# Quarter tiles of the input's block sums at a pitch of 320 columns, and five buffers instead of six in the weight rings

## The chip, the cores and the metric

The kernel runs on one core of one Trainium2 chip. The metric is the device time of one execution in microseconds (us). TensorE (PE in the profile) multiplies matrices, VectorE (DVE), ScalarE (ACT) and GpSimd (POOL) do elementwise work, and SyncE (SP) issues nearly all DMA transfers. Each engine has an instruction stream of its own, which it works off in order; semaphores order the streams against each other. On-chip memory has two parts: SBUF, the working memory of all engines, in which each of the 128 partitions holds a row of bytes, and PSUM, into which TensorE writes its sums.

## The reference

One step of a one-layer streaming encoder, for a prompt of 512 frames and a sample of 32 frames of a running stream. Both go through the layer as one matrix of 544 columns (`T`). Cut to what matters:

```python
xn   = rmsnorm(h, norm_g)
proj = xn @ w_in            # 1024 -> 3*2048 + 8 + 4*1024 + 2*1024 columns
u, v_m, z_m, ig, fg, q_h, f_h, i_h, g_h, ga, gb = split(proj)
c  = silu(causal_conv(u))                       # mLSTM branch, 4 heads of 512
qm, km = c @ w_qm, c @ w_km * 512 ** -0.5       # per head
hm = mlstm(qm, km, v_m, ig, log_sigmoid(fg), C0, n0, m0)
ya = ((layernorm(hm) + m_skip * c) * silu(z_m)) @ w_brm
oh = hgrn(silu(q_h), f_h, i_h, S0)              # HGRN2 branch, 8 heads of 128
yb = (rmsnorm(oh) * silu(g_h)) @ w_brh
h  = h + (sigmoid(ga) * ya + sigmoid(gb) * yb) @ w_out
h  = h + sigmoid(h @ w_pg) * (p @ w_ple)
y  = rmsnorm(h, final_g)                        # and the new states
```

All of it is in float32, and the states are outputs too.

## The kernel before

**Products.** A float32 product is made of three passes over operands that are split into a high and a low part (`fp32r`): high times high, high times low, low times high. So each weight piece of 128 x 512 (four weight blocks of 128 x 128) exists three times in SBUF: as it was loaded (`wr`, "raw"), its high part (`wh`, a copy by ScalarE) and its low part (`wl`, raw minus high by VectorE). Each kind has a ring of buffers, `NRAW` and `NPIECE` of them, six each. A ring is handed out when the program is built: a new piece takes a buffer that an older piece has given up, and the instruction that fills it waits until the older piece's last reader is done. For a raw piece that is a DMA in SyncE's queue, for a high piece a copy on ScalarE, for a low piece a subtraction on VectorE.

**Seven products for eight.** The big projection `w_in` and the output product `w_out` run over pairs of 128-column units (`class Two`; `Onto` for `w_out`) by Strassen's scheme in Winograd's form: seven block products, called a11, s2, a12, s3, s1, a22, s4, in place of eight. Each is 12 matmuls of 272 columns (four weight blocks, three passes each; 272 is `TH`, half of 544). Four of the seven (s1, s3, a22, s2) multiply with sums of blocks of the input. Those sums are made once, by `xf_sums` (line 365): for each of four pairs of input rows one tile of high parts and one of low parts, each with four quarters of 272 columns. Quarter 0 is for s1, 1 for s3, 2 for a22 and 3 for s2 (`moving`, line 528). The other three products read halves of the normalized input itself (`xh`, `xl`).

**Memory.** The rings and tiles are laid out in SBUF pool by pool, in the order of the lines at the function's head: constants `cp`, weight rings `wp`, the pair tiles `xp`, slots `sp`, small tiles `tp`. The pair tiles have two rings (tags x0 and x1) of four buffers, each of 4352 bytes per partition before, which is four quarters of 1088 bytes. In the built program the first of them begins 224 bytes past a multiple of 256, and 4352 and the sizes before it keep that for all eight. So the quarters begin 224, 32, 96 and 160 bytes past a multiple of 256. The same tiles hold other operands at other times (`pair_tile`, line 141): the raw input at the start, the first head's queries, the HGRN2 output ahead of `w_brh` and `h` ahead of `w_pg`; there the high part takes the first half and the low part the second.

**Stages.** Start and first projections (to about 60 us in the profile); four mLSTM heads (to about 590 us), each with keys and queries (`stage_k`, `stage_q`), scores, the chain of memory and output (`mchain`) and the product with `w_brm` (`stage_br`), between which a `Pump` places the blocks of the next projections; eight HGRN2 heads (to about 880 us), whose chain of levels is interleaved with further blocks; the merge gates; then `w_brh`, `w_out`, `w_pg` and the output.

**What sets the order.** TensorE's order is written out by hand from beginning to end. At the start and in the HGRN2 stage ScalarE's and VectorE's are too. In the mLSTM heads, in the merge's tail and for SyncE throughout, a scheduler that runs when the program is built places the instructions; it knows the rings, so a different number of buffers makes a different order. Once built, the order is fixed.

In the heads, the weights of a block are split three blocks ahead (`AHEAD`), and the results of a block leave PSUM through `keep` (line 563, a copy on ScalarE, names t...) or `put` (line 569, on VectorE or ScalarE). For the units of the convolution input `u` the target is a tile `ub`, whose convolution starts on ScalarE (`conv_first`, line 764) and goes on with three taps on VectorE (`conv_rest`, line 772, names cv...).

Of the kernel before, what the change touches and what calls it, by code (L numbers as in the profile page):

```python
# [20 lines left out]
NP = 512  # L21
T = NS + NP
TH = T // 2
MH = 4
HD = 512
KH = HD // P
# [27 lines left out]
NSLOT = 26  # L54
NEVAC = 8
WP = 512
NRAW = 6
NSUM = 4
NPIECE = 6
AHEAD = 3  # L60
SCRATCH = 1024
RAWAHEAD = 3
# [18 lines left out]
def hybrid_step(ctx: ExitStack, tc: tile.TileContext, a, o):  # L81
# [2 lines left out]

    cp = ctx.enter_context(tc.tile_pool(name="cp", bufs=1))
    wp = ctx.enter_context(tc.tile_pool(name="wp", bufs=NPIECE))
    xp = ctx.enter_context(tc.tile_pool(name="xp", bufs=KD // 2))
    sp = ctx.enter_context(tc.tile_pool(name="sp", bufs=NSLOT))
    tp = ctx.enter_context(tc.tile_pool(name="tp", bufs=2))
    psum = {}  # L90

    def aux_pool(name, bufs):
# [47 lines left out]

    def pair_tile(name, ring):

        t = xp.tile([P, 2 * T], F32R, tag=f"x{ring}", name=name)
        return t[:, :T], t[:, T:]

    def psplit(src, name, ring):
        hi, lo = pair_tile(name, ring)
# [117 lines left out]
    def rms_cols(acc, blocks, name, pc=None):  # L265

        pc = pc or paux(name + "pc")
        n = len(blocks)
        st = small("rms_s", [P, 8])
        V.memset(st[:, :n], 1.0)  # L270
        for i, (t0, m) in enumerate(blocks):
            PE.matmul(pc[:m, 0, 2 * i : 2 * i + 2], acc[:, t0 : t0 + m], ones, start=True, stop=True)
        i = 0
        while i < n:
            j = i
            while j < n and blocks[j][1] == blocks[i][1]:
                j += 1
            m = blocks[i][1]
            V.tensor_scalar(st[:m, i:j], pc[:m, 0, 2 * i : 2 * j : 2], 1.0 / D, EPS, ALU.mult, ALU.add)
            i = j  # L280
        r = small("rms_r", [P, 8])
        rsqrt(r[:, :n], st[:, :n], P, n)
        return r
# [81 lines left out]
    def xf_sums(k):  # L365

        ring = f"x{int(k in (1, 2))}"
        h = xp.tile([P, 4, TH], F32R, tag=ring, name=f"xfh{k}")
        l = xp.tile([P, 4, TH], F32R, tag=ring, name=f"xfl{k}")
        u = cp.tile([P, T], F32, tag="lm", name=f"xu{k}")  # L370
        x11, x12 = u[:, one], u[:, other]
        x21, x22 = (tp.tile([P, TH], F32, tag="half", name=f"xv{k}{b}", bufs=3) for b in range(2))
# [596 lines left out]
    def stage_q(h, u):  # L969
# [21 lines left out]
        if u:  # L991

            with tc.issue_after(read.ins):
                S.activation(small("silu", [1, 2]), ident[:1, :2], AF.Silu)
        return low

    def stage_scores(h):
# [327 lines left out]
    def hgrn_bounds(decayed, masked):  # L1325

        l0, l1 = vec[:, V_LB : V_LB + HH], vec[:, V_LB + HH : V_LB + 2 * HH]
        lm, le = small("lbm", [P, HH]), small("lbe", [P, 2, HH])
        with tc.issue_after(masked.ins):
            V.tensor_tensor(lm, l0, l1, ALU.max)  # L1330
            V.tensor_tensor(le[:, 0, :], l0, lm, ALU.subtract)
# [834 lines left out]
```

## Time and profile before

| | |
|---|---|
| three timed runs | 1117.81, 1118.29, 1118.54 us, median 1118.29 |
| profiled execution, first to last instruction | 1116.3 us |
| TensorE busy | 1108.7 us (99%), 8825 matmuls (8507 in the program; a product of plain float32 shows as two) |
| VectorE, ScalarE, GpSimd busy | 922.1, 714.8, 158.4 us |
| granted TensorE clock | 1.000 |
| DMA | 135.78 MB, mean 122 GB/s |

The profile has only the span of its execution; that execution's own time is not listed apart from it. The median of the timed runs is 2.0 us above the span, which is what lies before the first and after the last instruction. "Busy" counts the time from an instruction's start to its end. Matmuls overlap in the pipeline: one takes about 290 ns from start to end, but the next starts about 125 ns after it. So a TensorE that is 99% busy can still run slower or faster, and the time from one start to the next is what has to be read. In the timeline view a row is: start in us, duration in us, engine, line, operation, tiles written and read, shape, count, and in brackets the idle time ahead of it and what ended that.

### The profile page before, as it was taken

How to read it: one execution, taken by the hardware profiler on the slowest of the kernel's cores; microseconds unless marked ns; L12 is line 12 of the kernel's file. 1: busy time of each engine (PE TensorE's matmuls, PEld its weight loads, DVE VectorE, ACT ScalarE, POOL GpSimd, SP SyncE). 2: the span in 40 equal slices, each digit the busy share in tenths (PEclk: the TensorE clock that was granted, in tenths of full speed). 3: DMA queues.
4: the chain of work that ended last, by engine and by line, in shares of the span. 5: the costliest groups of instructions: out<-in, count | busy, mean ns of one | idle time of the engine just before them, and what ended most of it. 6: DMA issues, size and time to landing. Idle time of an engine off the chain costs nothing.

```text
span 1116.3 us, 23756 instructions
## 1 busy us (share of the span) xinstructions
PE 1108.7 (99%) x8825; PEld 1097.3 (98%) x8825; DVE 922.1 (83%) x1969; ACT 714.8 (64%) x1583; POOL 158.4 (14%) x412
## 2 busy tenths in 40 slices
PE   9999999999999999999999999999999999999998
PEld 9999999999999999999999999999999999999998
DVE  6986998676896786986898699999999888789785
ACT  6686657754666555664667478787777776445662
POOL 5112021101010110101200123222322000000000
PEclk9999999999999999999999999999999999999999
DMA  6234225232264132461556322122222353333943
GB/s 224 77 95 128 86 67 176 96 114 96 74 215 157 39 124 104 131 222 53 195 176 206 107 77 83 56 84 74 84 75 74 109 166 114 111 125 103 304 150 119
DMA packets 78044, 135.78 MB, mean 122 GB/s; under 512 B 8804, under 2 KB 16612, under 8 KB 77928
## 3 DMA queue, kind: packets, MB, share of 16 engines
q1 hardware_dynamic: 77760, 134.21, 36.9%
q8 instruction: 69, 1.13, 0.4%
q14 instruction: 47, 0.39, 0.1%
q10 hardware_dynamic: 168, 0.06, 0.0%
HBM read 109.32 MB, written 24.91 MB: 120 GB/s over the span
## 4 chain that ended last, share of the span: by engine, by line
PE 94%; DVE 3%; ACT 1%; DMA 1%; issue 1%; SPq 0%; ACTq 0%; DVEq 0%
PE d L549 42%; PE ya L199 9%; PE pg L2017 4%; PE yb L199 4%; PE k L199 4%; PE q L199 4%; PE C L1069 3%; PE pl L1741 3%; PE u L326 2%; PE sc L1012 2%; PE v L199 2%; PE nm L1248 2%; PE d L431 1%; PE ple L199 1%; PE yt L1290 1%; PE ho L1855 1%
## 5 line engine op out<-in xcount | busy, mean ns | idle before, releaser
L566 ACT COPY t<-d 128x272 f32<-128x272 f32 x126 | 47.4, 376 | 5.2 <-PE d L549 5.0
L1762 DVE TENSOR_TENSOR hkq<-hkq,hq 128x288 f32<-128x288 f32 (+1 forms) x96 | 41.5, 439 | 5.6 <-PE pl L1741 2.5
L1696 ACT COPY km<-hkq 128x256 f32<-128x256 f32 x56 | 23.9, 427 | 30.5 <-DVE hkq L1762 28.4
L1741 PE MATMUL pl<-hkq,km 128*128 128x128 f32 x224 | 37.9, 291 | 0.6 <-ACT km L1696 0.6
L774 DVE SCALAR_TENSOR_TENSOR cv<-ub,vec,cv 128x547 f32<-128x547 f32 x48 | 37.0, 781 | 0.4
L1741 PEld LDWEIGHTS pl<-hkq,km 128*128 128x128 f32 x224 | 30.9, 190 | 2.7 <-ACT km L1696 1.6
L1177 DVE SCALAR_TENSOR_TENSOR c<-c,wi,Cs 128x258 f32<-128x258 f32 x32 | 15.1, 477 | 20.2 <-PE Cs L1175 20.1
L1081 ACT COPY Co<-C 128x258 f32<-128x258 f32 x30 | 9.8, 379 | 28.3 <-PE C L1069 20.7
L1316 DVE TENSOR_TENSOR y<-ya,y 128x272 f32<-128x272 f32 x48 | 18.8, 432 | 8.8 <-PE ya L199 8.7
L1776 DVE COPY_PREDICATED at<-lmask,pl 128x256 f32<-128x256 uint8 (+1 forms) x56 | 25.3, 452 | 0.3
L1259 ACT COPY y<-nm 128x516 f32<-128x516 f32 x16 | 9.4, 589 | 18.0 <-PE nm L1248 17.8
L1026 ACT CAST sh<-dm 128x512 fp32r<-128x512 f32 (+3 forms) x16 | 7.4, 459 | 20.4 <-DVE dm L1020 20.4
L939 POOL COPY vsm<-vt 128x96 f32<-128x96 f32 x16 | 7.2, 462 | 87.4 <-ACT vt L577 44.3
L1069 PE MATMUL C<-vh,kwh 128*128 128x258 f32 x96 | 19.3, 283 | 0.0
L1069 PE MATMUL C<-vh,kwl 128*128 128x258 f32 x96 | 19.3, 282 | 0.0
L1069 PE MATMUL C<-vl,kwh 128*128 128x258 f32 x96 | 19.3, 282 | 0.0
L1012 PE MATMUL sc<-q,kh 128*128 128x512 f32 (+3 forms) x80 | 18.6, 320 | 0.1
L1207 DVE BATCH_NORM_STATS2 bs<-y 128x6 f32<-128x512 f32 (+1 forms) x20 | 13.7, 687 | 5.1 <-ACT y L1259 5.0
L963 DVE TENSOR_TENSOR kl<-kf,kh 128x512 fp32r<-128x512 f32 x16 | 11.0, 686 | 8.1 <-ACT kh L962 8.0
L767 POOL COPY uo<-ub 128x3 f32<-128x3 f32 x16 | 7.6, 472 | 64.1 <-DVE ub L573 39.3
L1248 PE MATMUL nm<-vh,sh 128*128 128x258 f32 x80 | 16.5, 288 | 0.0
L1768 POOL TENSOR_TENSOR hq<-hq 128x136 f32<-128x136 f32 (+4 forms) x40 | 16.0, 399 | 3.1
(4666 smaller groups left out, 5119.2 us busy)
## 6 DMA issues: line engine op xcount, KB each, us to landing
ya_d<-y SPq DMA_DIRECT2D x32, 272.0 KB, 3.0
y<-ya_d SPq DMA_DIRECT2D x24, 272.0 KB, 3.8
c<-in_C SPq DMA_DIRECT2D x16, 258.0 KB, 4.5
out_Cs<-c SPq DMA_DIRECT2D x16, 258.0 KB, 2.8
out_Cp<-Co SPq DMA_DIRECT2D x15, 258.0 KB, 2.4
x<-in_xT SPq DMA_DIRECT2D x8, 272.5 KB, 4.7
ya<-ya_d SPq DMA_DIRECT2D x8, 272.0 KB, 4.8
h<-in_xT SPq DMA_DIRECT2D x8, 272.0 KB, 2.8
```

The costliest lines, as they stand in the source:

```text
L199: PE.matmul(both[b][:m, :TH], part(w, off + k * step, m, x), xx[:, half(b)], start=(k == 0 and j == 0), stop=(k == n - 1 and j == 2),)
L549: PE.matmul(ps, ww[:, c], xx, start=(start and k == 0 and j == 0), stop=end, skip_group_check=not start,)
L566: S.copy(t, ps)
L774: last = V.scalar_tensor_tensor(cv[:, :547], ub[:, j : j + 547], vcol(V_CW + 4 * ft + j), cv[:, :547], ALU.mult, ALU.add)
L1012: PE.matmul(pn[:, 0, :n], ks[f][x][:, j * P : (j + 1) * P], qs[f][y][:, NS + j * P : T], start=(f == 0 and i == 0), stop=(f == KH - 1 and ...
L1069: PE.matmul(pn[g][:, :VH], kw[b][x][:, f * P : (f + 1) * P], vv[b][y][:, g * VH : (g + 1) * VH], start=(b == 0 and j == 0), stop=(b == NB ...
L1248: PE.matmul(pn[:, g, :VH], st[j][x][:, (i - j) * P : (i - j + 1) * P], vv[j][y][:, g * VH : (g + 1) * VH], start=(j == 0 and q == 0), stop ...
L1696: S.copy(km.rearrange("p (n j c) -> p n j c", j=2, c=c), view(kk, HB, ((2 * c, NA // (2 * c)), (c - HB, 2), (1, c))),)
L1741: PE.matmul(pn[:, b * P : (b + 1) * P], km[:, b * P : (b + 1) * P], view(qq, b * P, ((2 * c, P // (2 * c)), (HB + c, 2), (1, c))), start=True,
L1762: V.tensor_tensor(x, x, t, ALU.mult)
L1776: V.copy_predicated(at[:, :n], lmask[:, li, :n], pn[:, :n])
L2017: PE.matmul(ps, part(w, k * P, P, x), xx[:, c], start=(k == 0 and j == 0), stop=(k == KD - 1 and j == 2))
```

## The change

Quarters of the block sums get a pitch of 320 columns (1280 bytes) instead of 272; only 272 of the 320 are used. The pair tiles become 5120 bytes for it, 8 x 768 = 6144 bytes more per partition. The three weight rings give up one buffer of 2048 bytes each, which is 6144 bytes too. A tile of 48 columns (192 bytes), used by nothing, stands between the weight rings and the pair tiles, and four small tiles get one buffer instead of two. In the built program the first pair tile now begins 160 bytes past a multiple of 256, and since 1280 and 5120 are multiples of 256, so does each quarter of each of the eight tiles. Where a pair tile holds a high and a low half, they stay back to back, so their four halves begin at 160, 224, 32 and 96 instead of 224, 32, 96 and 160. The weight rings keep their place (224 past a multiple of 256).

```diff
+TW = 320
...
-NRAW = 6
+NRAW = 5
...
-NPIECE = 6
+NPIECE = 5
...
     wp = ctx.enter_context(tc.tile_pool(name="wp", bufs=NPIECE))
+    gp = ctx.enter_context(tc.tile_pool(name="gp", bufs=1))
     xp = ctx.enter_context(tc.tile_pool(name="xp", bufs=KD // 2))
...
+    gp.tile([P, 48], F32, name="gap")
...
     def pair_tile(name, ring):
 
-        t = xp.tile([P, 2 * T], F32R, tag=f"x{ring}", name=name)
-        return t[:, :T], t[:, T:]
+        t = xp.tile([P, 4 * TW], F32R, tag=f"x{ring}", name=name)
+        return t[:, :T], t[:, T : 2 * T]
...
-        st = small("rms_s", [P, 8])
+        st = small("rms_s", [P, 8], bufs=1)
...
-        h = xp.tile([P, 4, TH], F32R, tag=ring, name=f"xfh{k}")
-        l = xp.tile([P, 4, TH], F32R, tag=ring, name=f"xfl{k}")
+        h = xp.tile([P, 4, TW], F32R, tag=ring, name=f"xfh{k}")[:, :, :TH]
+        l = xp.tile([P, 4, TW], F32R, tag=ring, name=f"xfl{k}")[:, :, :TH]
...
-                S.activation(small("silu", [1, 2]), ident[:1, :2], AF.Silu)
+                S.activation(small("silu", [1, 2], bufs=1), ident[:1, :2], AF.Silu)
...
-        lm, le = small("lbm", [P, HH]), small("lbe", [P, 2, HH])
+        lm, le = small("lbm", [P, HH], bufs=1), small("lbe", [P, 2, HH], bufs=1)
```

No instruction is added or removed, and the order of the 8507 matmuls that the program issues is the same. On VectorE, ScalarE, GpSimd and SyncE the order differs in the mLSTM heads and around the merge's tail. In the built program's order the rows below read: line, operation, tile written <- tiles read with their buffer numbers, elements. The changed file's line numbers are three higher there, and its buffer numbers four.

The first place is on VectorE, among the projections that run beside the end of the second head (`h` = 1), near 314 us of the profile. Names: `ws310` is the weight sum for block s3 of units 10 and 11 and `ws310l` its low part, `ws110l` that for s1; `ub8` and `ub10` are convolution tiles that take results from PSUM (`d81`, `d101`), `cv8` is a convolution tap, `hm7l` a low part of the head's output. Before:

```order
L175 TENSOR_TENSOR wa1210l_4624<-wi10r1_4464,wa1210h_4623 128x512
L482 TENSOR_TENSOR ws310_4643<-wi10r0_4371,wi11r0_4373 128x512
L138 TENSOR_TENSOR hm7l_4573<-c7_2856,hm7h_4572 128x544
L573 TENSOR_TENSOR ub8_4385<-d81_4384,t168_4462 128x272
L175 TENSOR_TENSOR ws310l_4646<-ws310_4643,ws310h_4645 128x512
L175 TENSOR_TENSOR ws110l_4664<-ws110_4576,ws110h_4663 128x512
L573 TENSOR_TENSOR ub10_4586<-d101_4585,t110_4604 128x32
L573 TENSOR_TENSOR ub10_4586<-d101_4585,t110_4604 128x240
L774 SCALAR_TENSOR_TENSOR cv8_4682<-ub8_4385,vec_80,cv8_4682 128x547
```

and now:

```order
L178 TENSOR_TENSOR wa1210l_4628<-wi10r1_4468,wa1210h_4627 128x512
L141 TENSOR_TENSOR hm7l_4577<-c7_2860,hm7h_4576 128x544
L485 TENSOR_TENSOR ws410_4631<-ws210_4582,wi10r1_4468 128x512
L576 TENSOR_TENSOR ub8_4389<-d81_4388,t168_4466 128x272
L485 TENSOR_TENSOR ws310_4647<-wi10r0_4375,wi11r0_4377 128x512
L576 TENSOR_TENSOR ub10_4590<-d101_4589,t110_4608 128x32
L576 TENSOR_TENSOR ub10_4590<-d101_4589,t110_4608 128x240
L777 SCALAR_TENSOR_TENSOR cv8_4686<-ub8_4389,vec_84,cv8_4686 128x547
L178 TENSOR_TENSOR ws310l_4650<-ws310_4647,ws310h_4649 128x512
L178 TENSOR_TENSOR ws110l_4668<-ws110_4580,ws110h_4667 128x512
```

The sum `ws310` moved behind the first read of `d81`, and both reads of `d101` and a convolution tap moved ahead of `ws310l` and `ws110l`. The same rows moved in the same way in the third head for units 14 and 15 (`ws314l`, `ub12`, `ub14`, `cv12`).

The second place is on VectorE too, in the first head's queries near 88 us. `kl` are low parts of the keys, `q0` and `q1` those of the queries (each a read of PSUM), `col` and `cols` copies of small transposes out of PSUM, `wq010l` and `wq011l` the low parts of the next query weights, and `emc` a small copy that is needed later. Before:

```order
L963 TENSOR_TENSOR kl010_1204<-kf01_1200,kh010_1203 128x512
L989 TENSOR_TENSOR q0_1298<-q0001_1273,q0_1298 128x272
L989 TENSOR_TENSOR q0_1298<-q0000_1272,q0_1298 128x272
L963 TENSOR_TENSOR kl011_1235<-kf01_1200,kh011_1234 128x512
L175 TENSOR_TENSOR wq010l_1396<-wq01r0_1391,wq010h_1395 128x512
L175 TENSOR_TENSOR wq011l_1400<-wq01r512_1393,wq011h_1399 128x512
L904 COPY col_1358<-cols_1336 128x72
L906 COPY cols_1360<-cols_1336 96x12
L989 TENSOR_TENSOR q1_1330<-q0011_1305,q1_1330 128x272
L989 TENSOR_TENSOR q1_1330<-q0010_1304,q1_1330 128x272
```

and now:

```order
L907 COPY col_1362<-cols_1340 128x72
L909 COPY cols_1364<-cols_1340 96x12
L1205 COPY emc_2036<-col_1362 128x4
L1205 COPY emc_4118<-col_1362 128x4
L1206 COPY emc_2036<-cols_1364 32x1
L1206 COPY emc_4118<-cols_1364 32x1
L992 TENSOR_TENSOR q0_1302<-q0000_1276,q0_1302 128x272
L992 TENSOR_TENSOR q1_1334<-q0011_1309,q1_1334 128x272
L992 TENSOR_TENSOR q1_1334<-q0010_1308,q1_1334 128x272
L178 TENSOR_TENSOR wq010l_1400<-wq01r0_1395,wq010h_1399 128x512
L178 TENSOR_TENSOR wq011l_1404<-wq01r512_1397,wq011h_1403 128x512
```

The two weight splits moved from ahead of `col` to behind it, behind the `emc` copies and behind three reads of query results.

## The prediction

> **What bounds the kernel now.** I read the page's busy times first, then the chain of work that ended last, then the timeline of TensorE, to see whether its 99% are useful.
>
> ```profile
> span 1116.3 us, 23756 instructions
> PE 1108.7 (99%) x8825; PEld 1097.3 (98%) x8825; DVE 922.1 (83%) x1969; ACT 714.8 (64%) x1583; POOL 158.4 (14%) x412
> ...
> PE 94%; DVE 3%; ACT 1%; DMA 1%; issue 1%; SPq 0%; ACTq 0%; DVEq 0%
> PE d L549 42%; PE ya L199 9%; PE pg L2017 4%; PE yb L199 4%; PE k L199 4%; PE q L199 4%; PE C L1069 3%; PE pl L1741 3%; PE u L326 2%; PE sc L1012 2%; PE v L199 2%; PE nm L1248 2%; PE d L431 1%; PE ple L199 1%; PE yt L1290 1%; PE ho L1855 1%
> ```
>
> TensorE sets the end: 94% of the chain is its own, 42% the matmuls of line 549, which are the blocks of the seven-product scheme. So the time changes in two ways only: a matmul takes another time from start to start, or TensorE waits where it did not. The change bears on both. It moves the operands of line 549, and it reorders VectorE and ScalarE, which feed TensorE with weights.
>
> **Part 1: where the quarters lie.** Every one of these blocks is 12 matmuls of 272 columns. I took all blocks whose 12 matmuls follow each other without another line between them and without a wait, from the first start to the start of the next block, and let the profile add them up. First s1 (20 blocks), then s3 (14), a22 (23) and s2 (15): the first block of s1 and the four sums.
>
> ```profile
> 167.10:168.62 1.52, 1.52 (x14) 1.52 (x13) 1.00 0.00 0
> sum 30.15, PE 30.15 PEld 30.15; mean PE 1.51 PEld 1.51
> ...
> sum 21.22, PE 21.22 PEld 21.22; mean PE 1.52 PEld 1.52
> ...
> sum 34.94, PE 34.94 PEld 34.94; mean PE 1.52 PEld 1.52
> ...
> sum 22.27, PE 22.27 PEld 22.27; mean PE 1.48 PEld 1.48
> ```
>
> The sums give 1507.5, 1515.7, 1519.1 and 1484.7 ns a block (30.15/20, 21.22/14, 34.94/23, 22.27/15), at a granted clock of 1.00 (the third column from the end). The four differ in nothing but the quarter they read. s1 reads quarters 224 bytes past a multiple of 256, s3 32, a22 96, s2 160. s2 is the fast one by 22.8, 31.0 and 34.4 ns. Is that the address, or something in s2? In `w_out` the same four products read slots of another pitch, where s2 has no such place. There s2 (four blocks) and a22 (four) are:
>
> ```profile
> sum 6.03, PE 6.03 PEld 6.03; mean PE 1.51 PEld 1.51
> ...
> sum 6.00, PE 6.00 PEld 6.00; mean PE 1.50 PEld 1.50
> ```
>
> 1507 and 1500 ns, so s2's lead is gone and turned round. I take it that the address does it, and after the change all four quarters begin at 160. The gain is 22.8 + 31.0 + 34.4 = 88.2 ns for each pair of units. There are 42 pairs on `w_in`: 18 in the mLSTM heads, 16 in the HGRN2 heads, 8 for the merge gates. That is 3.70 us if all of it shows. In the HGRN2 heads the blocks alternate with a chain of levels through VectorE, which is busy for 88% there, and a TensorE that is early may only wait for the next level:
>
> ```profile
> 600.00:870.00 270.00, 269.23 (x2154) 265.75 (x2153) 237.72 (x516) 202.34 (x494) 67.03 (x154) 1.00 0.28 90
> ...
> ACT km L1696 <- DVE hkq L1762: 28.4, 30, 2.6
> ```
>
> So 26 pairs (2.3 us) are sure and 16 (1.4 us) are not; I take 0.3 us of these. The pair tiles with high and low halves turn from 224, 32, 96, 160 to 160, 224, 32, 96. With the high half read twice, the four means above (125.6, 126.3, 126.6 and 123.7 ns a matmul, a twelfth of the block) give 754.1 ns for six matmuls before and 751.5 after. That is 0.4 ns each, for some 1056 matmuls (384 in `w_brh`, 384 in `w_pg`, 288 at the start) 0.4 us. The slots move too, without an aim; I take 0 for them. **Term 1: -3.0 us**, with ends of 0 (the address is not the cause) and -4.1.
>
> The Trainium skill, "TensorE: Matmul & The Clock Gate", section "Back-to-back issue gap", has the gap of warm matmuls as columns / 2.4 + 2.5 ns, with no word on addresses, which is 115.8 ns for 272 columns wherever they lie. By it this term would be 0, and the sum below 3.0 us more. The trace has 123.7 to 126.6 ns in one and the same shape, so it speaks against the rule.
>
> **Part 2: five buffers.** A piece now waits for the last reader of the fifth piece before it, not of the sixth. In the HGRN2 heads, where the order is by hand, a copy for a block five ahead waits for the block that TensorE has just ended, four blocks of about 1.5 us before its own use and that is some 6 us of room against 0.6 for a copy and 0.7 for a subtraction. So the ring itself costs nothing. What costs is the order that the scheduler makes of it, in three places.
>
> At the first, VectorE now has both reads of `d101` and a convolution tap ahead of `ws310l`, and the weight sum behind the read of `d81`.
>
> ```profile
> 313.74 0.44 DVE L573 TENSOR_TENSOR ub<-d,t 128x272 f32<-128x272 f32 x1 [0.20 <-PE d L549]
> 314.09 0.68 DVE L175 TENSOR_TENSOR ws310l<-ws,ws310h 128x512 fp32r<-128x512 f32 x1
> 314.69 0.68 DVE L175 TENSOR_TENSOR ws110l<-ws,ws110h 128x512 fp32r<-128x512 f32 x1
> 315.30 0.50 DVE L573 TENSOR_TENSOR ub<-d,t 128x32 f32<-128x32 f32 x2
> 315.71 0.78 DVE L774 SCALAR_TENSOR_TENSOR cv<-ub,vec,cv 128x547 f32<-128x547 f32 x1
> 316.41 0.68 DVE L175 TENSOR_TENSOR wa2210l<-wi11r,wa2210h 128x512 fp32r<-128x512 f32 x1
> ```
>
> ```profile
> 314.90 0.29 PE L549 MATMUL d<-xh,wa1210l 128*128 128x272 f32 x1
> 315.03 0.29 PE L549 MATMUL d<-xfh,ws310h 128*128 128x272 f32 x1
> 315.15 0.28 PE L549 MATMUL d<-xfl,ws310h 128*128 128x272 f32 x1
> 315.28 0.29 PE L549 MATMUL d<-xfh,ws310l 128*128 128x272 f32 x1
> ```
>
> `d101` is the block of `wa1210`; its last matmul ends at 314.90 + 0.29 = 315.19, so the two reads can't start before, and stand at 315.30 as in the row. They take 0.41 to the next start, the tap 0.70, and `ws310l` comes where `wa2210l` stands, at 316.41, and is ready at 317.09. TensorE wanted it at 315.28, its third matmul of the block: 1.8 us late. On ScalarE the tap's first step now precedes `ws310h` too, a shorter delay that lies inside the 1.8. Behind `ws310l` the next pieces follow by 0.6 us, faster than TensorE's 1.5 us a block, so it stops once.
>
> The third head has the same rows:
>
> ```profile
> 464.75 0.29 PE L549 MATMUL d<-xfh,ws314l 128*128 128x272 f32 x1
> ...
> 465.88 0.68 DVE L175 TENSOR_TENSOR wa2214l<-wi15r,wa2214h 128x512 fp32r<-128x512 f32 x1
> ```
>
> 465.88 + 0.68 - 464.75 = 1.8 us again. The third place is the first head's queries:
>
> ```profile
> 88.00 0.23 DVE L904 COPY col<-cols 128x72 f32<-128x72 f32 x1 [0.56 <-PE cols L902]
> 88.15 0.16 DVE L906 COPY cols<-cols 96x12 f32<-96x12 f32 x1
> 88.23 0.78 DVE L989 TENSOR_TENSOR q<-q,q 128x272 fp32r<-128x272 f32 x2
> 88.92 0.88 DVE L922 TENSOR_TENSOR dm<-bc,cmask 128x128 f32<-128x128 f32 x4
> ...
> 89.97 0.15 DVE L1202 COPY emc<-col 128x4 f32<-128x4 f32 x1
> 90.04 0.13 DVE L1203 COPY emc<-cols 32x1 f32<-32x1 f32 x1
> ```
>
> ```profile
> 88.49 0.29 PE L199 MATMUL q<-cs0h,wq010l 128*128 128x272 f32 x1
> ```
>
> `col` waits for TensorE's transposes and so stays at 88.00. From 88.23 come four `emc` copies of 0.07 each (90.04 - 89.97), to 88.51, then three query reads of 0.345 (half of 88.92 - 88.23), to 89.54, then `wq010l`, ready at 90.22. TensorE wanted it at 88.49: 1.7 us late. So far 1.8 + 1.8 + 1.7 = 5.3 us.
>
> Other places are moved by less. One I followed is `wbm001l`:
>
> ```profile
> 171.12 0.68 DVE L175 TENSOR_TENSOR wbm001l<-wbm00r,wbm001h 128x512 fp32r<-128x512 f32 x1
> 171.85 0.44 DVE L573 TENSOR_TENSOR ub<-d,t 128x272 f32<-128x272 f32 x1
> 172.20 0.78 DVE L774 SCALAR_TENSOR_TENSOR cv<-ub,vec,cv 128x547 f32<-128x547 f32 x1
> ...
> 173.65 0.41 PE L199 MATMUL ya<-hm2h,wbm001l 128*128 128x272 f32 x2
> ```
>
> Now behind that read and that tap, it starts at 172.90 and is ready at 173.58, 0.07 us ahead of its use instead of 1.85: no wait, but no reserve either. For all such places I put an estimate of 0.9 us, half of one place like the three, with ends of 0 and 1.8. **Term 2: +6.2 us**, ends 0 and 7.1.
>
> **Sum.** -3.0 + 6.2 = +3.2 us. The span would be 1116.3 + 3.2 = 1119.5, and with the 2.0 us by which the median lies above it, **1121.5 us**, 0.29% slower.
>
> **The rivals.** *The waits are absorbed* (faster). TensorE stops at the three places, but wherever it waits anyway further on in the same head, VectorE has meanwhile caught up and that wait shrinks. Its idle time of 7.6 us (1116.3 - 1108.7) bounds it. If 5.3 us go that way, 1118.3 - 3.0 + 0.9 = 1116.2; with the whole gain of 4.1 and no small places, 1114.2. I name 1115.3. It decides for faster from some 5.4 us absorbed. Against it: the idle time is spread over the run, and two of the three places lie in the midst of a dense stretch.
>
> *The address is not the cause* (slower still). Then term 1 is 0: 1118.3 + 6.2 = 1124.5. The four sums speak against it.
>
> *One place or two don't bite* (no change). The order is certain, but each price supposes that VectorE and ScalarE arrive as in the trace of before; it waits for TensorE ahead of each (0.20 and 0.56 us idle), so it can't come much earlier. Without one place: 1121.5 - 1.8 = 1119.7.
>
> *The raw ring stops VectorE* (slower). A raw piece now lands later by a load behind its buffer's last reader, and a sum that waits for it holds all of VectorE's queue, reads of PSUM too. In the third head `wi25r` is to follow a query weight, `wq21r`, whose last read is just ahead of that sum. The loads and that piece:
>
> ```profile
> wi33r<-in_w_in SPq DMA_DIRECT2D x2, 256.0 KB, 2.6
> wq00r<-in_w_qm SPq DMA_DIRECT2D x2, 256.0 KB, 4.9
> ```
>
> ```profile
> 352.25 0.75 DVE L175 TENSOR_TENSOR wq211l<-wq21r,wq211h 128x512 fp32r<-128x512 f32 x1
> ```
>
> ```profile
> 365.31 0.29 PE L199 MATMUL q<-cs10h,wq211l 128*128 128x272 f32 x1
> ```
>
> A load takes 2.6 to 4.9 us, but TensorE reads what VectorE makes there 365.31 - 353.00 = 12.3 us later. If a hold in two heads still costs 1.3 us each, an estimate of half a load: 1124.
>
> **How the numbers follow.** Forecast 0.45, absorbed 0.15, not the address 0.12, fewer places 0.2, raw ring 0.08. What a measurement of this kernel can tell from no change is about 0.2%, here 1116.05 to 1120.5. The forecast's own range, 1120 to 1123, lies nearly all on the slower side, as do the second and last rivals: 0.42 + 0.12 + 0.08, and a little of the others, 0.64 slower. Fewer places gives most of the 0.22 for the same, absorption the 0.14 for faster. The range reaches to the outer rivals, 1115.5 to 1125.0.
>
> **What would show it.** The sums of s1, s3 and a22 should fall to s2's 1485 ns a block. TensorE should be idle 1.7 to 1.8 us at the first `ws310l`, `ws314l` and `wq010l`, with VectorE as the releaser, and nowhere new in the HGRN2 heads. I am wrong if the blocks stay apart, or if those three waits are missing or taken back by the end of their head.

## The result, and the profile after

The changed kernel takes 1127.13 us (median of four runs, 1126.46 to 1127.36), against 1118.41 us before on the same chips: a ratio of 1.0079 (95% interval 1.0067 to 1.0091), 8.7 us slower. The forecast was 1121.5 us with a range to 1125.0. The direction was right, the size was not, and the time lies outside the range.

The page of the changed kernel, busy times and the chain of work that ended last:

```profile
span 1125.4 us, 23815 instructions
PE 1111.0 (99%) x8825; PEld 1096.2 (97%) x8825; DVE 921.6 (82%) x1969; ACT 715.5 (64%) x1583; POOL 156.7 (14%) x412
...
PE 84%; DVE 11%; issue 2%; ACT 1%; DMA 1%; SPq 0%; DVEq 0%; ACTq 0%
```

The span grew by 9.1 us. TensorE's share of the chain fell from 94% to 84%, and VectorE's rose from 3% to 11%: TensorE now waits for it. TensorE's own waits, by the line that waits and the one waited for (us in total, times, longest). Left out are those that stand in the kernel before as well, such as 1.1 us of `warm` for `emc` at the top:

```profile
...
PE ya L202 <- DVE y L1319: 1.0, 1, 1.0
PE d L552 <- DVE ws310l L178: 0.8, 1, 0.8
PE d L552 <- DVE ws314l L178: 0.8, 1, 0.8
...
PE q L202 <- DVE wq010l L178: 0.7, 1, 0.7
PE q L202 <- DVE q L992: 0.6, 1, 0.6
PE d L552 <- ACT ws314h L177: 0.6, 1, 0.6
PE d L552 <- ACT ws310h L177: 0.6, 1, 0.6
```

All three forecast places are in it, and one that was not named: `ya` waiting for `y`.

Since the order of the matmuls is the same in all kernels here (apart from seven repeated ones in one experiment), the same matmul can be looked up in each timeline, and the difference of its starts tells how late TensorE is by then. For example the first matmul of `wa2210`, before and after:

```profile
318.05 0.29 PE L549 MATMUL d<-xfh,wa2210h 128*128 128x272 f32 x1
```

```profile
324.15 0.28 PE L552 MATMUL d<-xfh,wa2210h 128*128 128x272 f32 x1
```

The changed kernel is 6.10 us late there. The table has this lateness in us against the profile of before, for the change and for experiments that follow (e1: rings at five without the change of the quarters; e3: the high ring alone; e6: raw and low rings; e9: high and low rings; e4: first head two ahead; e8: e4 with the order mended). A single profile scatters: in the first row, ahead of all places that the change moves, the kernels lie up to 1.0 us apart.

| matmul of | place | start before | after | e1 | e3 | e6 | e9 | e4 | e8 |
|---|---|---|---|---|---|---|---|---|---|
| wk000h | first keys | 68.37 | 0.40 | -0.07 | 0.49 | 0.93 | -0.07 | 0.46 | 0.81 |
| wi330h | behind the first head's queries | 102.60 | 3.43 | 3.06 | 4.47 | 3.58 | 3.11 | 0.08 | 0.42 |
| wa114h | | 147.90 | 3.50 | 3.18 | 4.57 | 4.12 | 3.22 | 0.56 | 0.43 |
| wbm010h | behind wbm001l | 177.67 | 4.40 | 4.07 | 5.44 | 3.98 | 4.14 | 1.51 | 1.10 |
| ws48h | ahead of ws310 | 312.03 | 4.01 | 4.37 | 5.01 | 3.80 | 3.67 | 1.06 | 0.45 |
| wa2210h | behind ws310l | 318.05 | 6.10 | 6.46 | 7.13 | 4.20 | 5.76 | 3.17 | 1.45 |
| ws412h | ahead of ws314 | 461.50 | 6.00 | 6.87 | 6.84 | 4.71 | 5.50 | 2.76 | 2.57 |
| wa2214h | behind ws314l | 467.52 | 8.10 | 8.98 | 9.01 | 4.75 | 7.62 | 4.86 | 3.60 |
| wbm321h | ahead of the last output product | 611.79 | 8.09 | 9.28 | 9.73 | 5.35 | 8.54 | 4.45 | 3.57 |
| wbm331h | in it | 617.82 | 9.47 | 10.53 | 9.72 | 5.35 | 8.53 | 5.76 | 3.97 |
| wa1188h | end of the HGRN2 heads | 861.78 | 9.76 | 10.82 | 10.05 | 5.56 | 8.85 | 6.04 | 4.19 |
| wple10h | end of the merge gates | 948.88 | 9.05 | 10.81 | 10.07 | 5.56 | 8.85 | 5.31 | 3.48 |
| wp000h | w_pg | 1049.84 | 8.89 | 10.84 | 10.09 | 5.54 | 8.88 | 5.20 | 3.36 |

**The blocks.** The same sums as in the prediction, over all undisturbed blocks: s1 (20), s3 (12), a22 (24) and s2 (16).

```profile
sum 29.70, PE 29.70 PEld 29.70; mean PE 1.49 PEld 1.49
...
sum 17.88, PE 17.88 PEld 17.88; mean PE 1.49 PEld 1.49
...
sum 35.56, PE 35.56 PEld 35.56; mean PE 1.48 PEld 1.48
...
sum 23.70, PE 23.70 PEld 23.70; mean PE 1.48 PEld 1.48
```

That is 1485, 1490, 1482 and 1481 ns a block, where s1, s3 and a22 had 1508, 1516 and 1519. The three forms fell to s2's time, as forecast.

**The queries.** TensorE's rows, and then its clock (the third column from the end) in stretches of 1 us:

```profile
88.30 0.39 PE L202 MATMUL q<-cs0h,wq010h 128*128 128x272 f32 x1
89.33 0.39 PE L202 MATMUL q<-cs0h,wq010h 128*128 128x272 f32 x1 [0.65 <-DVE q L992]
...
90.62 0.55 PE L202 MATMUL q<-cs0h,wq010l 128*128 128x272 f32 x2 [0.66 <-DVE wq010l L178]
90.98 0.65 PE L202 MATMUL q<-cs1h,wq010h 128*128 128x272 f32 x2
91.43 0.66 PE L202 MATMUL q<-cs1l,wq010h 128*128 128x272 f32 x2
...
95.01 0.41 PE L202 MATMUL q<-cs0l,wq010h 128*128 128x272 f32 x2
95.26 0.42 PE L202 MATMUL q<-cs0h,wq010l 128*128 128x272 f32 x2
```

```profile
88.00:89.00 1.00, 0.67 (x7) 1.00 0.91 315
89.00:90.00 1.00, 0.64 (x3) 1.00 0.20 75
90.00:91.00 1.00, 0.38 (x3) 0.98 0.00 0
91.00:92.00 1.00, 1.00 (x7) 0.50 0.12 16
92.00:93.00 1.00, 1.00 (x6) 0.50 0.94 326
93.00:94.00 1.00, 1.00 (x6) 0.50 0.48 182
94.00:95.00 1.00, 1.00 (x8) 0.81 0.00 0
```

Two waits stand where one was forecast, 1.7 us together by the starts. Behind them the granted clock is 0.50 from about 90.96 to 94.38 (the 0.98 and the 0.81 give the ends): 3.4 us at half the clock. A pair of matmuls starts every 0.45 us in it (91.43 - 90.98) and every 0.25 us behind it (95.26 - 95.01), so another 1.5 us is lost (3.4 x 0.20 / 0.45). This was in no term of the prediction. Stop and half clock together make 3.2 us; the table has 3.0 from the first keys to `wi330h`.

**The weight sums.** VectorE, then TensorE, at `ws310l`:

```profile
319.47 0.51 DVE L576 TENSOR_TENSOR ub<-d,t 128x32 f32<-128x32 f32 x2 [0.33 <-PE d L552]
319.89 0.78 DVE L777 SCALAR_TENSOR_TENSOR cv<-ub,vec,cv 128x547 f32<-128x547 f32 x1
320.59 0.68 DVE L178 TENSOR_TENSOR ws310l<-ws,ws310h 128x512 fp32r<-128x512 f32 x1
```

```profile
319.15 0.28 PE L552 MATMUL d<-xh,wa1210l 128*128 128x272 f32 x1
320.04 0.39 PE L552 MATMUL d<-xfh,ws310h 128*128 128x272 f32 x1 [0.61 <-ACT ws310h L177]
...
321.32 0.39 PE L552 MATMUL d<-xfh,ws310l 128*128 128x272 f32 x1 [0.76 <-DVE ws310l L178]
```

Reads, tap and `ws310l` follow each other as the prediction laid them out. The third matmul of the block was due 0.13 + 0.25 us behind 319.15, at 319.53, and starts at 321.32: 1.8 us, as forecast. The blocks around it lose 0.3 more (table: 4.01 to 6.10), and the same 2.1 stand at `ws314l`.

**The place not named.** In the fourth head's last output product VectorE stands 4.41 us in front of a raw weight that has not landed, and a read of PSUM stands behind it:

```profile
623.65 0.69 DVE L510 TENSOR_TENSOR ws<-wi64r,wi64r 128x512 f32<-128x512 f32 x1 [4.41 <-DMA wi64r<-in_w_in]
624.98 0.78 DVE L1319 TENSOR_TENSOR y<-ya,y 128x272 f32<-128x272 f32 x2
```

```profile
625.56 0.64 PE L202 MATMUL ya<-hm12h,wbm330h 128*128 128x272 f32 x2 [1.03 <-DVE y L1319]
```

TensorE can't start the next product until that read has freed its PSUM: 1.4 us in the table (8.09 to 9.47). Before, VectorE waited 1.30 us for the same piece and TensorE not at all:

```profile
609.99 0.69 DVE L507 TENSOR_TENSOR ws<-wi64r,wi64r 128x512 f32<-128x512 f32 x1 [1.30 <-DMA wi64r<-in_w_in]
```

### The profile page after: what moved, and what is told of

It is laid out like the page before. It is cut to its first block, busy times and chain, and to the rows that moved or that the text cites. A ratio compares the mean times of both kernels' runs of the same rounds, so it can differ in the third digit from the quotient of the medians.

```text
span 1125.4 us, 23815 instructions
## 1 busy us (share of the span) xinstructions
PE 1111.0 (99%) x8825; PEld 1096.2 (97%) x8825; DVE 921.6 (82%) x1969; ACT 715.5 (64%) x1583; POOL 156.7 (14%) x412
## 4 chain that ended last, share of the span: by engine, by line
PE 84%; DVE 11%; issue 2%; ACT 1%; DMA 1%; SPq 0%; DVEq 0%; ACTq 0%
PE d L552 36%; PE ya L202 7%; PE q L202 4%; PE pg L2020 4%; PE yb L202 4%; PE k L202 4%; PE C L1072 4%; PE sc L1015 3%; PE u L329 2%; PE v L202 2%; PE nm L1251 2%; PE pl L1744 2%; DVE hkq L1765 2%; DVE ws L510 1%; PE d L434 1%
## 5 line engine op out<-in xcount | busy, mean ns | idle before, releaser
L960 ACT ACTIVATE kf<-k 128x272 f32<-128x272 f32 x32 | 11.0, 392 | 11.8 <-PE k L202 11.8
L942 POOL COPY ksm<-kf 128x96 f32<-128x96 f32 x16 | 7.7, 479 | 66.7 <-ACT kf L960 66.6
```

## Experiments

The theory after the result: two effects add. Five buffers make an order in which TensorE stops (some 11 us, with the clock), and the new place of the quarters gives part of that back.

**e1: the rings alone.** Kernel before with `NRAW = 5` and `NPIECE = 5`.

> Kernel before with five buffers in all three weight rings and nothing else: quarters at 272 columns, on 224, 32, 96 and 160 past a multiple of 256 as before. Theory (two effects that add: the rings' order costs some 11 us, the addresses give back some 2.6 to 3.7): all stops of the changed kernel are here (first head's queries with the clock at half behind them, ws310l, ws314l, the second and last output product), the blocks s1, s3, a22 are at 1507, 1516, 1519 ns and s2 at 1485 again, and the time is 1127.1 + 2.6 to 3.7 = 1129.7 to 1130.8 us. Rival (the wider pair tiles are what stops TensorE, the rings nothing): 1118.4 us, no new stop.

1129.03 us, ratio 1.0106 (1.0090 to 1.0121), span 1127.1. The blocks are at 1508, 1518, 1518 and 1483 ns, and every stop is there. The rings cost 10.8 us of span. On VectorE, ScalarE and GpSimd the order of e1 is that of the change but for one instruction, so the two differ by the place of the quarters. The quarters give back 1.7 us by the spans (1127.1 to 1125.4), and 2.5 us by the medians, each against before on its own chips (11.2 and 8.7 us slower): less than the 2.6 to 3.7 expected by the one, close to its lower end by the other. The table shows where. Between `wk000h` and `wbm321h` the change loses 7.7 us and e1 9.35; of these 1.7 us, 0.7 lies at one place near 257 us, where e1 waits for `vt` and the change doesn't. In the HGRN2 heads both lose the same 0.3 (9.48 to 9.76 between their first block and wa1188h in the one, 10.51 to 10.82 in the other), so nothing shows there. Over the merge gates the change falls by 0.71 and e1 by 0.01, which is the whole 8 x 0.089. That the spans differ by only 1.7 us comes for the most part from the first row: the change's profile is 0.5 us behind e1's there already, and the kernels with e1's quarters lie between -0.07 and 0.93 in that row.

**e3: the high ring alone; e6: raw and low; e9: high and low.** The first two edits (e9 has `NPIECE = 5` alone):

```diff
-        hi = wp.tile([P, WP], F32R, tag="wh", name=name + "h")
+        hi = wp.tile([P, WP], F32R, tag="wh", name=name + "h", bufs=5)
```

```diff
-NRAW = 6
+NRAW = 5
...
-        lo = wp.tile([P, WP], F32R, tag="wl", name=name + "l")
+        lo = wp.tile([P, WP], F32R, tag="wl", name=name + "l", bufs=5)
```

(Both times the same again where `split_piece` takes its buffers.)

> Kernel before with five buffers in the ring of the high parts alone (raw and low six, quarters as before). Theory (the order that follows from the high ring costs nearly all): ScalarE's order is that of five in all rings, stops at the first head's queries, ws310l and ws314l, 1129 to 1131 us. Rival (each ring carries a third): about 1122 us. Rival (raw or low ring): 1118 to 1120 us.

> Kernel before with five buffers in the raw and the low ring and six in the high ring; quarters as before. Theory (the high ring makes the order that stops TensorE at ws310l and ws314l; the queries' place suffers from any ring): a stop at the first head's queries of 2 to 4 us with its clock, next to none at ws310l and ws314l (0.4 each), 1120.5 to 1124 us. Rival (any ring of five does all of it): 1129 us or more. Rival (only all three together): 1118.4 us.

> Kernel before with five buffers in the high and low rings and six in the raw ring; quarters as before. It differs from e1 by one raw buffer. Theory (the raw ring delays the load of wi64r and VectorE stands behind it): VectorE waits under 1.5 us for wi64r in place of 4.3, the stop of 1.3 to 1.4 us in the third head's last output product is gone, the stops at ws310l and ws314l stay; span 1127.1 - 1.3 = 1125.8 us, time about 1127.5 us. Rival (the high and low rings delay it): 4.3 us and the stop as in e1, 1129 us.

e3 took 1128.21 us (1.0093, 1.0078 to 1.0108; a little below the range), e6 1123.77 (1.0051, 1.0037 to 1.0065), e9 1127.09 (1.0080, 1.0063 to 1.0097; span 1125.2). The high ring alone costs nearly all, and ScalarE's order in e3 is that of e1 to the last instruction. One thing makes e3 look dearer than it is: in its profile the half clock behind the queries lasts 6.8 us and not 3.4 (0.50 from about 89.3 to 96.1). The stops at `ws310l` and `ws314l` belong to the high ring: 2.1 us each in e3 and e9, while e6 loses 0.4 and nothing there (and 0.4 at the block behind each). The queries stop in all three. The stop at `wbm331` (of the fourth head; the expectation of e9 calls it the third) is in e1 (1.25) and in none of e3, e6 and e9. Between e1 and e9 stands one raw buffer, and VectorE's wait at that piece:

```profile
620.16 0.69 DVE L507 TENSOR_TENSOR ws<-wi64r,wi64r 128x512 f32<-128x512 f32 x1 [1.53 <-DMA wi64r<-in_w_in]
```

1.53 us in place of 4.3. So the stop needs the raw ring at five, and, since e6 doesn't have it, the order of the high ring at five as well. e9's span is 1.9 us below e1's, where 1.3 were expected; another 0.7 lies near 257 us, at the wait that of these two only e1 has.

**e4: the first head two ahead.** Changed kernel, only the pieces beside the first head made later:

```diff
+            self.src, self.rawahead, self.ahead = src, RAWAHEAD, AHEAD
...
-                self.prepare(i + 1 + AHEAD)
+                self.prepare(i + 1 + self.ahead)
...
-        pump.rawahead = 0
+        pump.rawahead, pump.ahead = 0, 2
```

> Changed kernel, but the blocks that run beside the first head have their weights split two blocks ahead in place of three; rings, addresses and the other heads as in the change. Theory (the stop at the first head's queries comes from the order there, and the clock at half behind it from the stop): wq010h and wq010l are in time, no stop at 88 to 91 us, the granted clock stays at 1.00, the time is 1127.1 - 1.7 (stop) - 1.7 (clock) = 1123.7 us. Rival (the clock falls there whatever TensorE waits for): 1125.4 us with the clock at half near 91 us. Rival (the stop only moves on): 1127 us.

1122.41 us (1.0043, 1.0028 to 1.0058), span 1121.9: 3.5 below the change by span, and 4.7 by the medians, since the profiled execution is the longest of its four. The expectation was 1123.7. The table has 0.08 behind the queries in place of 3.43, and TensorE's clock over the place is full:

```profile
85.00:100.00 15.00, 15.00 (x117) 1.00 0.46 139
```

The traces of the two differ in the place of 12 of VectorE's instructions, 13 of ScalarE's and 2 of GpSimd's, so the order of these few rows cost the 3.4 us there. All four executions of e4 have a mean granted clock of 0.999 or 1.000, all four of the change 0.998: without the stop there is no half clock. Whether work in the stop keeps it away too is the next run.

**e5: work in the stop.** Changed kernel with the first query matmul repeated:

```diff
+                    if name == "q010" and (k, j, b) == (0, 0, 0):
+                        for _ in range(7):
+                            PE.matmul(both[b][:m, :TH], part(w, off, m, x), xx[:, half(b)], start=True, stop=True)
```

> Changed kernel; at the place where TensorE stops in the first head's queries the first matmul of the third query product runs eight times in place of once (seven more, 0.9 us, each started anew, so the sums are the same). They fill the first half of the stop; the weight wq010l is as late as before. Theory (the clock at half comes from too little work in a stretch, light transposes and the stop together): TensorE waits 0.8 us less at the first place, the granted clock stays at 1.00, the time is 1127.1 - 1.7 = 1125.4 us (up to 1126.2, since the second product's result is read a little later). Rival (the clock falls for another reason): the clock is at half near 91 us as before, 1127.1 us or more.

1125.85 us (1.0068, 1.0055 to 1.0082), span 1123.3, 2.1 below the change.

```profile
87.75 1.16 PE L204 MATMUL q<-cs0h,wq010h 128*128 128x272 f32 x7
...
90.08 0.52 PE L205 MATMUL q<-cs0h,wq010l 128*128 128x272 f32 x2 [0.65 <-DVE wq010l L178]
```

```profile
89.00:90.00 1.00, 0.43 (x4) 1.00 0.01 5
90.00:91.00 1.00, 0.92 (x7) 1.00 0.00 0
91.00:92.00 1.00, 1.00 (x10) 1.00 0.65 227
```

TensorE still waits for `wq010l`, and the clock stays at 1.00. Between the first keys and `wi330h` this profile loses 1.5 us where the change loses 3.0. More work, less time, but not in each execution: two of the four have a mean clock of 1.000 and 0.999 and spans of 1123.3 and 1122.1, the other two have 0.998, as the change has, and 1125.2 and 1125.0 (a mean doesn't tell where the clock fell). The median is 1.3 us below the change, which the two intervals don't tell apart. So e5's profile shows what the half clock costs, 1.5 us, and its four executions that seven matmuls keep it away at times only. e2 (below), which has the change's order and its stop, also has two executions at 0.998 and two at 1.000, and there the spans don't follow the clock (1126.4 and 1128.8, 1127.2 and 1127.0). And in e10, of the same order and with the same two waits (0.64 and 0.65), the half clock lasts 6.8 us and the place costs 4.3. One stop thus brings no such stretch, one or two of them. That it comes from too little work in the stretch ahead fits e4 and e5's profile, and what decides in a single execution is open. The waits of 0.61 and 0.76 at `ws310` are as long and bring no half clock in the profile. There full matmuls surround them, while at the queries 21 transposes of 4 columns stand ahead of the waits; that these count as little work is argued, not shown. The Trainium skill, "TensorE: Matmul & The Clock Gate", section "What's actually happening", has a free-running window of about 3.4 us and the half clock after at least one idle window. The length agrees with the 3.4 us measured; "idle" does not, since TensorE was busy for 0.38 to 0.67 of each of the last three microseconds ahead. A window that runs free of the program would let one stop have different results, as in e2 and e5, but no run tests that.

**e2: all quarters at 96.** Changed kernel, only the pair tiles moved, by 64 bytes:

```diff
-    gp.tile([P, 48], F32, name="gap")
+    gp.tile([P, 32], F32, name="gap")
+    gq.tile([P, 16], F32, name="gap2")
```

(`gq` is a pool behind the pair tiles.)

> Changed kernel with the unused tile 16 columns narrower and 16 unused columns behind the pair tiles, so that only the pair tiles move, by 64 bytes: all four quarters begin 96 past a multiple of 256, pitch 320 as in the change, the order of every engine is the changed kernel's. Theory (the start modulo 256 decides): all four kinds of block at a22's old 1519 ns, 34 ns more each, 136 ns for a pair of units; with the 26 pairs outside the HGRN2 heads 1127.1 + 3.5 = 1130.6 us, with all 42 pairs 1132.8 us. Rival (the wider pitch, or equal residues, make the blocks fast): blocks stay at 1482 to 1490 ns and the time at 1127.1 us.

The blocks s1 (20), a22 (24) and s2 (16):

```profile
sum 30.34, PE 30.34 PEld 30.34; mean PE 1.52 PEld 1.52
...
sum 36.47, PE 36.47 PEld 36.47; mean PE 1.52 PEld 1.52
...
sum 24.30, PE 24.30 PEld 24.30; mean PE 1.52 PEld 1.52
```

1517, 1520 and 1519 ns: all are slow, s2 too. The place is the cause, and neither the pitch nor equal residues are. But the time missed: 1128.83 us (1.0104, 1.0087 to 1.0121), 1.7 above the change where 3.5 to 5.7 were expected, and 1.0 by span (the profiled execution is the shortest of its four). Over the merge gates 1.0 us shows, of 8 x 0.136 = 1.1, and `w_brh` and `w_pg`, which read halves of the same tiles, take 0.4 and 0.3 us more. In the mLSTM heads next to nothing shows: 0.3 us more than the change between `wk000h` and `wbm321h`, where 18 pairs would make 2.4. In this profile the wait of `ya` for `y` is missing, since `wi64r` had landed by 623.02, and that alone took back 1.0 us. A TensorE that is early or late by a microsecond meets other waits, and waits that end by a DMA don't move with it.

**e10: the weights moved; e11: quarters at 128.** Changed kernel with a 16-column tile ahead of the weight rings and the gap smaller by as much (e10), or with the pair tiles 32 bytes lower (e11):

```diff
+    gw = ctx.enter_context(tc.tile_pool(name="gw", bufs=1))
     wp = ctx.enter_context(tc.tile_pool(name="wp", bufs=NPIECE))
...
-    gp.tile([P, 48], F32, name="gap")
+    gw.tile([P, 16], F32, name="gap1")
+    gp.tile([P, 32], F32, name="gap")
```

> Changed kernel with the three weight rings moved by 64 bytes (32 in place of 224 past a multiple of 256) and the unused tile behind them smaller by as much, so that nothing else moves; the order of every engine is the changed kernel's. Theory (only where the moving operand starts counts): s1, s3, a22 and s2 stay at 1481 to 1490 ns a block. Rival (the distance between weights and moving operand counts): all four at about 1517 ns, as with the quarters at 96. Time as the changed kernel's, 1127 us, or 1128.8 us.

> Changed kernel with only the pair tiles moved, by 32 bytes: all quarters begin 128 past a multiple of 256; the order of every engine is the changed kernel's. Theory (a narrow good start at 160): the four kinds of block at 1500 to 1520 ns. Rival (a wide good stretch around 160): 1481 to 1490 ns.

e10, s1, a22 and s2:

```profile
sum 30.33, PE 30.33 PEld 30.33; mean PE 1.52 PEld 1.52
...
sum 36.47, PE 36.47 PEld 36.47; mean PE 1.52 PEld 1.52
...
sum 24.31, PE 24.31 PEld 24.31; mean PE 1.52 PEld 1.52
```

The theory fell and its rival holds. The quarters had not moved from 160, only the weights, from 224 to 32, and all blocks are at 1517 to 1520 ns. What counts is the distance between moving operand and weights, modulo 256: 160 - 224 = 192 is fast, 160 - 32 = 128 is as slow as e2's 96 - 224 = 128. In e11 the distance is 160: a22 1480, s2 1481, s1 1488 and s3 1506 ns, so the fast stretch reaches down to 160 for three of the four, and that theory fell too. That one and the same distance gives 1480 to 1506 shows that something beside it counts there. The single times, 1130.53 and 1125.92 us, are not weighed.

**e12: the distance without a wider pitch.** Kernel before with the quarters where they were, and the weights of s1, s3 and a22 moved inside longer buffers:

```diff
+START_AT = {"ws1": 16, "ws3": 32, "wa22": 48, "ws2": 0}
...
+        t = wp.tile([P, 2 * WP + 64], F32R, tag="whl", name=name + "p")
+        at = max([c for n, c in START_AT.items() if name.startswith(n) and len(name) > len(n)], default=0)
+        low_of[name] = t[:, at + WP : at + 2 * WP]
+        return t[:, at : at + WP], low_of[name]
```

(The joined ring has six buffers; `NRAW = 5`; the first head is two ahead as in e4.)

> Kernel before (quarters at 272 columns, on 224, 32, 96 and 160) with six buffers that hold a high and a low part together, 256 bytes longer, in which the weights of s1, s3, a22 and s2 begin 64, 128, 192 and 0 bytes in, so that each quarter lies 192 past its weights modulo 256; five raw buffers, and the first head's blocks split two ahead. Theory (the distance between moving operand and weights decides, as the moved weights of e10 showed): s1, s3, a22 and s2 all at 1481 to 1490 ns a block without a wider pitch; no stop at the first head's queries; time 1118.4 - 1.9 (what the same gain brought between e1 and the change) + 0 to 2 for the five raw buffers and the joined ring: 1116.5 to 1118.5 us. Rival (the absolute place of the quarters counts too): s1, s3, a22 at 1500 ns or more and 1118.5 to 1121 us.

s1 (20), s3 (14), a22 (24) and s2 (16):

```profile
sum 29.78, PE 29.78 PEld 29.78; mean PE 1.49 PEld 1.49
...
sum 20.78, PE 20.78 PEld 20.78; mean PE 1.48 PEld 1.48
...
sum 35.69, PE 35.69 PEld 35.69; mean PE 1.49 PEld 1.49
...
sum 23.76, PE 23.76 PEld 23.76; mean PE 1.48 PEld 1.48
```

1489, 1484, 1487 and 1485 ns with the old pitch: the distance is confirmed from the other side. The time is 1120.23 us (1.0021, 1.0012 to 1.0030), not the 1116.5 to 1118.5 expected. Against the profile of before it is ahead by up to 0.6 us until 405 us and behind by up to 0.3 from there to 545, so the mLSTM heads return little of what their blocks gain. At 557 us before itself waits 0.69 us, and e12 is 1.2 ahead. Then it loses 2.3 us up to 570, where TensorE waits for VectorE's low parts of the fourth head's values and for the new memory. The merge gates return the whole 8 x 0.082 (1.5 us behind at their start, 0.85 at their end). No run separates the joined ring from the five raw buffers there.

**e7: what the runs before it pointed to.** Changed kernel with the high ring back at six, the low and raw rings at five, e4's edit, and quarters at columns 0, 320, 640 and 920 of 1216:

```diff
-TW = 320
+XW, QUARTER = 1216, (0, 320, 640, 920)
...
-NPIECE = 5
+NPIECE = 6
...
-        lo = wp.tile([P, WP], F32R, tag="wl", name=name + "l")
+        lo = wp.tile([P, WP], F32R, tag="wl", name=name + "l", bufs=5)
```

> Changed kernel with six buffers in the high ring, five in raw and low, the first head's blocks split two ahead, and the quarters of a pair tile at columns 0, 320, 640 and 920 of 1216 (starts 160, 160, 160 and 0 past a multiple of 256; 4864 bytes for a tile). Theory: no stop at the first head's queries, at most 0.4 us at ws310l and ws314l; s1, s3 and a22 at 1485 ns, s2 at about 1504; a pair gains 88 - 19 = 69 ns, 26 pairs 1.8 us, all 42 pairs 2.9 us; 1118.4 - 1.8 to - 2.9, and up to 0.8 back: 1115.5 to 1117.4 us, faster than both. Rival (raw or low ring stops VectorE somewhere): 1119 us or more.

1119.17 us (1.0013, 1.0004 to 1.0022): the expectation failed, the kernel is not faster than before, and the time is the rival's. s1, s3 and a22 are at 1485, 1491 and 1482 ns and s2, now at distance 32, at 1506, as expected. But it is ahead of before by only 1.3 us at 312 us, and gives back 0.8 around `ws310`, 0.9 around `ws314` and 0.6 at `wbm331`.

**e8: the order mended at five buffers.** e4 with these edits at the two places:

```diff
-                conv(h + 1)
+                high, low = made[f"ws3{(h + 1) * KH + 2}"]
+                with tc.issue_after(high.ins), tc.issue_after(low.ins):
+                    conv(h + 1)
...
+            late = self.unit in (10, 14)
+            with tc.issue_after(made[f"ws3{self.unit}"][1].ins) if late else nullcontext():
+                self.put(0, 0, ps, self.t["t1"], "add")
```

(and the read of `d81` or `d121` behind the sum `ws310` or `ws314` in the same way.)

> The kernel with the first head two ahead (e4), and at two places the order mended by hand: the sums ws310 and ws314 stand ahead of the read of d81 (d121), ws310l and ws314l ahead of the reads of d101 (d141) and of the convolution's first step and taps. Rings (five each) and addresses as in the change. Theory (the order makes these stops, not the wait for a buffer): the low parts come 0.7 to 1.2 us late in place of 2.0, or not at all; the time falls from e4's by 1.6 to 4 us, to 1118.5 to 1121 us. Rival (with five buffers the copy ws310h or ws310l waits for its buffer, whatever the order): the stops stay at 1.9 to 2.1 us, 1122.4 us.

1121.08 us (1.0025, 1.0015 to 1.0034), span 1119.8, 2.1 below e4 by span and 1.3 by the medians, where at least 1.6 was expected. The stops fall from 2.1 to 1.0 us each, with 0.4 more at the block behind each, which e4 had not. This profile gives back 1.5 us near 407 us, where TensorE waits 1.03 us for `vt` on VectorE; e4 loses 0.3 there. What is left:

```profile
314.56 0.68 DVE L485 TENSOR_TENSOR ws<-wi10r,wi11r 128x512 f32<-128x512 f32 x1
...
315.93 0.69 DVE L178 TENSOR_TENSOR ws310l<-ws,ws310h 128x512 fp32r<-128x512 f32 x1 [0.34 <-ACT ws310h L177]
```

```profile
315.27 0.62 ACT L177 CAST ws310h<-ws 128x512 fp32r<-128x512 f32 x1 [2.11 <-DVE ws L485]
```

ScalarE's copy waits for the sum on VectorE, which stands behind another sum and a low part; the profile names no buffer as the last to come. So a third to a half of each stop is shown to be the order of these few rows. The rest seems to lie in VectorE's queue ahead of the sum, which this run didn't change.

## Why the prediction was wrong

The step that failed is in term 2: the order of five buffers was priced at 6.2 us with an upper end of 7.1, and it costs 10.8 by span (e1). The half clock behind the queries' stop was in no term, and the "small places" were put at a fifth of what they are.

**Term 2, the stops.** In the terms of the sum, from e1 and the change:

- `ws310l` and `ws314l`: 1.8 each forecast, 1.8 each measured at the block itself, with 0.3 more around each that fall to the small places. The reads, the tap and the low part stand in the order that was laid out from the rows.
- the first head's queries: 1.7 forecast, 3.0 to 3.1 measured. The stop was 1.7, but the half clock behind it was missed.
- "small places", 0.9 forecast as half of one stop, 4.1 measured in e1 (10.8 - 1.8 - 1.8 - 3.1): `wbm001l` 0.9 where 0.07 us of reserve was reckoned, the hold at `wi64r` 1.3 to 1.4, 0.7 near 257 us in e1 alone, 0.6 around `ws310l` and `ws314l`, 0.4 near 586 us, and 0.3 to 0.6 near 407 us. The upper end of 1.8 stood on no row.

**Term 1, the addresses.** Forecast -3.0 us. Measured between e1 and the change: -1.7 by the spans, -2.5 by the medians against before, -2.4 by the table from `wk000h` to `wp000h` (1.95 us apart there, and 0.47 the other way round at the start). The intervals of the two ratios, 1.3 and 1.7 us to each side, don't tell -2.5 from -3.0. The price of a pair was right (88.2 ns forecast, 89 measured), but three parts of the sum were not:

- "26 pairs are sure" holds for the merge gates, which returned all of their 0.7 us. For the heads it is not shown: 1.7 us came there, and 0.7 of it at a wait and not at blocks. In e2 and e12 the heads passed on little of what their blocks lost or gained.
- the 0.3 us for the HGRN2 heads did not come.
- the 0.4 us for the high and low halves did not come either: from first to last matmul `w_brh` takes 48.08 us before and 48.09 now, `w_pg` 49.33 and 49.40. With the quarters at 96 or the weights moved (e2, e10) they take 48.5 and 49.7, so places count there too, but the four means of the blocks don't give their price.

The reason given, the address of the quarter, was half of it: what counts is its distance from the weights. Here both say the same, because the weight rings did not move.

**The sum.** The span came out 5.9 us above the 1119.5 of the forecast: 4.6 from term 2 (small places 3.2, half clock 1.4) and, by the spans, 1.3 from term 1. The time is 5.6 above, since the 2.0 us between span and time was 0.3 too much: each execution's time lies 1.7 to 1.8 above its own span (1127.12 and 1125.4 for the profile of the change), and the 2.0 compared different executions.

**The rivals.** "The raw ring stops VectorE" had a chance of 0.08 and was looked for in the third head at `wi25r`. It came true as a mechanism at another piece, `wi64r`. That its price there, 1.4, is near the 1.3 named for one hold is luck: the 1.3 was half of a load's time. "Absorbed" and "fewer places" were wrong: each place bit, and no more than 0.2 to 0.6 us was taken back at a time (near 101, 304 and 551 to 557 us). "Not the address" was wrong.

**"The ring itself costs nothing"** held where the order is by hand: from `wbm331h` to `wa1188h` the change loses 0.3 us. At `wi64r` it did not hold: one raw buffer more took VectorE's wait from 4.3 to 1.5 us (e9 against e1).

## What to carry to other kernels

A buffer less in a ring changes what a scheduler does with all the work around it, so its price is read from the new order, piece by piece, with the queue that each late piece stands in, and every place has to be walked: the unnamed ones together cost 4.1 us, more than any named one. A short stop of TensorE can cost twice, once as a wait and again as half the clock: here 1.7 us and then some 1.4 more. A gain of a few nanoseconds a matmul arrives only in stretches where TensorE waits for nobody; where a chain or a DMA sets the end of a wait, it turns into waiting.

## What the runs showed of the hardware

Two things were not expected. In the blocks of the seven-product scheme, the time from start to start of a 272-column fp32r matmul depends on the distance, modulo 256 bytes, between its moving operand and its weights: 192 gives 1481 to 1491 ns for twelve, 0 and 32 give 1506 to 1508, 64 gives 1516 to 1518, 128 gives 1517 to 1520, and 160 is mixed (1480 to 1506). Moving the one by 64 bytes (e2) or the other the opposite way round (e10) does the same. Why is open, and the figures don't carry over to `w_brh` and `w_pg`.

And TensorE's clock fell to half for 3.4 us after waits of 1.3 us (by the profile) behind a row of 4-column transposes, though TensorE was never idle for a whole microsecond. Without the stop (e4) it stayed at full speed in all four executions. With the stop it did not fall in two of four (e2), it fell for 6.8 us in the profiles of e3 and e10, and seven more matmuls in the stop (e5) kept it up in two of four, which were 1.7 to 3.1 us shorter by span than the other two. How much work is too little is open.
